# The projections of two head groups share one PSUM sum behind the last head, and half of the norms move behind it

## The chip, the cores and the metric

The kernel runs on one core of a Trainium2 chip. That core has five engines that work side by side, each on its own queue of instructions: TensorE (PE in the profile, its weight loads PEld) multiplies matrices and writes to PSUM; VectorE (DVE), ScalarE (ACT) and GpSimd (POOL) work on elements; SyncE (SP) issues the DMAs. The metric is the device time of one execution in microseconds, the median of several runs.

## The reference

A transformer encoder of two layers, 1024 tokens of width 1024, float32. Each layer mixes four groups of four heads side by side, joins their outputs through one output matrix, and follows it by a gated MLP with a convolution over tokens:

```python
for l in range(DEPTH):
    h = rms_norm(x, mix_pre_gain[l])
    (a_q, a_k, a_v, b_cq, b_ckv, b_kr, c_q, c_k, c_v, d_q, d_k, d_v) = split_columns(h @ w_in[l])
    o_a = neighbourhood_attention_2d(...)       # group a: 2-D window, learned relative bias
    ...
    mixed = jnp.concatenate([o_a, o_b, o_c, o_d], axis=-1) @ w_out[l]
    x = x + rms_norm(mixed, mix_post_gain[l])
    h = rms_norm(x, ffn_pre_gain[l])
    y = conv_gated_mlp(h, w_up[l], conv_w[l], conv_b[l], w_down[l])
    x = x + rms_norm(y, ffn_post_gain[l])
```

`mixed` is a sum over the groups: 256 columns of the concatenation, times 256 rows of `w_out`, for each. The order in which the groups' shares are added is free.

## The kernel before

Every float32 product is made of three matmuls of 128x512 (`mm3`, lines 255 to 257): each operand is split into a high part that TensorE takes at full rate and the low rest, ACT casting the high part and DVE subtracting it; `whi`/`wlo`, `PTh`/`PTl` are such pairs.

A layer runs through the input projection, the sixteen heads (groups d, c, b, a in this order), a *tail*, the *gated* part and the *down* part. Within the heads nothing is ordered by hand instruction by instruction: each step is put on a list with a planned time (`self.at(t, f)`), the steps are issued in the order of those times, and the numbers of the table `P` set them. A head takes four slots of the planned length `LD`, `LC`, `LB` or `LA` (5.4 for group a).

In a slot of group a, PE makes scores (`s_a`), DVE adds the relative bias and takes maxima (`P_a`, `nm_a`, line 1096), ACT exponentiates, POOL multiplies by `rr_a` (line 1134), PE transposes (`pt_a`, line 1183), ACT and DVE split the result into `PTh_a` and `PTl_a` (line 1193), and PE multiplies by the values (`ob_mix`, line 1210). The bias table comes by small DMAs and two POOL operations (lines 1016 and 1018, `rel_bias`).

The output projection of a finished group runs among the next group's heads. For each of eight tiles of 128 tokens and each half of 512 columns, `out_group`'s `mm` puts six matmuls into a PSUM bank (`ob`, `oc`, `oa` or `pb_mix`), and its `add` lets DVE add them to the running sum `y` (line 828). So group b's share is added among the heads of group a. Group a's own share comes behind the last head, in `tail`.

`tail` takes the token tiles one after another. Per tile: matmuls and two adds; ACT squares `y`, POOL takes the power (line 86, `rs_p`), and `y` is multiplied by the post gain (line 303, on DVE, for tile 5 on POOL); DVE adds it to the residual (`xo`, line 309); ACT squares again, POOL takes the power (`rs_f`); DVE makes the normed row (line 717). Then `split` transposes it and splits it into the operands `B11`, `B21` and `B22` of the gated part (`fB`, lines 274 to 276).

The gated part multiplies by 22 tiles of the up weights, by a scheme of seven products (P1 to P7) in place of eight, like Strassen's. It needs sums of token tiles (`token_sums`, line 757) and, from these, four more operands T1 to T4 (`fT`). T1, T2 and T4 lie in a pool that is opened when the mixing pool is closed; B11 and B21 lie in two of four *shared places* (`share(2)`, `share(3)`) that all parts use in turn. The first weight tile runs in two halves of 256 columns, `halves`.

The down part loads the gated rows and the down weights from HBM in pieces (`rows`), each into a place as it comes free: shared places 1, 2 and 3, and `fx` and `fy` of a pool that follows the gated part's.

## Time and profile before

| | us |
|---|---|
| median of 3 runs (2689.8 to 2691.87) | 2690.39 |
| the profiled execution | 2694.25 |
| its span, first to last instruction | 2692.4 |

Times on the page and in the rows count from the start of the span. A layer takes some 1336 us, and the second repeats the first. In an answer of the trace the engine named in brackets is the one that released the waiting instruction last; names are those of the program with their numbers left out.

### The profile page before, as it was taken

To read this page: it belongs to the slowest core of one execution; us is meant where nothing else is said; L and a number is where in the kernel's file an instruction comes from. 1 tells how busy PE (TensorE), PEld (TensorE's weight loads), DVE (VectorE), ACT (ScalarE), POOL (GpSimd) and SP (SyncE) were. 2 spreads that over 40 slices of the span, in tenths; PEclk is the share of its full clock that TensorE was granted. 3 is DMA by queue.
4 is the path that set the end of the run, shared out by engine and by line. 5 is a ranking of instruction groups with operands and counts; after the bars stand their busy time and mean duration, and the time that the engine had idled before them with its cause. 6 is when DMAs were issued, how large, how long until landed. Compare 5 with 4: busy or idle time off the path is not lost. (4 is left out here: it accounts for less than half of the span.)

```text
span 2692.4 us, 40234 instructions
## 1 busy us (share of the span) xinstructions
PE 2565.2 (95%) x14533; PEld 2210.0 (82%) x14533; DVE 2111.1 (78%) x3099; ACT 1463.6 (54%) x2704; POOL 798.2 (30%) x761
## 2 busy tenths in 40 slices
PE   7999999997799999999999999999968999999998
PEld 7999888885688888788789998888757888888886
DVE  5347899989878888878854568999797778888787
ACT  5347677666544444544653466776664444454433
POOL 1343212264333343100234432112743333330001
PEclk9999999999899999999999999999988999999999
DMA  6343412234222222550352434122432222226502
...
DMA packets 316913, 268.00 MB, mean 100 GB/s; under 512 B 104762, under 2 KB 262570, under 8 KB 316714
## 3 DMA queue, kind: packets, MB, share of 16 engines
...
## 5 line engine op out<-in xcount | busy, mean ns | idle before, releaser
L1309 POOL TENSOR_TENSOR sums<-loads 128x512 f32<-128x512 f32 x84 | 170.0, 2023 | 153.0 <-DMA loads<-in_w_up 67.2
L1309 POOL TENSOR_TENSOR loads<-loads,sums 128x512 f32<-128x512 f32 x42 | 57.7, 1374 | 372.4 <-DVE wgl L1319 229.5
L1530 ACT CAST dhP<-rows 128x1024 fp32r<-128x1024 f32 x88 | 89.4, 1052 | 130.1 <-issue 53.7
L86 POOL TENSOR_TENSOR rs_pf<-rs_pf,mhalf 128x1 f32<-128x1 f32 x15 | 13.9, 928 | 467.7 <-ACT rs_pf L85 467.6
L1531 DVE TENSOR_TENSOR dlP<-rows,dhP 128x1024 fp32r<-128x1024 f32 x88 | 105.2, 1219 | 40.7 <-ACT dhP L1530 40.7
L255 PE MATMUL dx<-dhP 128*128 128x512 f32 x308 | 120.2, 390 | 1.1 <-DVE yfQ L1597 1.1
L257 PE MATMUL dx<-dhP,dlP 128*128 128x512 f32 x308 | 120.0, 389 | 0.0
L256 PE MATMUL dx<-dlP,dhP 128*128 128x512 f32 x308 | 119.8, 389 | 0.0
L1188 ACT CAST PTh_b<-pt_b 128x512 fp32r<-128x512 f32 x128 | 74.9, 587 | 57.6 <-PE pt_b L1183 56.5
L257 PE MATMUL ux<-fT,wql 128*128 128x512 f32 (+1 forms) x272 | 102.6, 377 | 0.0
L255 PE MATMUL pb_mix<-whi_wa,h 128*128 128x256 f32 x320 | 100.0, 313 | 0.1
L1376 ACT ACTIVATE c<-ug,cw 128x1024 f32<-128x1024 f32 x44 | 54.7, 1244 | 82.4 <-DMA gate<-c 79.4
L255 PE MATMUL ux<-fT,wqh 128*128 128x512 f32 (+1 forms) x256 | 96.9, 378 | 1.4 <-ACT fT L275 1.4
L1377 DVE SCALAR_TENSOR_TENSOR c<-ug,cw,c 128x1023 f32<-128x1023 f32 x44 | 56.8, 1291 | 51.4 <-ACT c L1376 51.4
L256 PE MATMUL ux<-fT,wqh 128*128 128x512 f32 (+1 forms) x256 | 96.5, 377 | 0.0
L1419 ACT ACTIVATE c<-c 128x1024 f32<-128x1024 f32 x44 | 46.7, 1062 | 85.7 <-DVE c L1379 85.7
L1193 DVE TENSOR_TENSOR PTl_c<-pt_c,PTh_c 128x512 fp32r<-128x512 f32 x128 | 85.5, 682 | 8.5 <-ACT PTh_c L1188 7.9
L1188 ACT CAST PTh_c<-pt_c 128x512 fp32r<-128x512 f32 x128 | 74.5, 587 | 32.4 <-PE pt_c L1183 30.6
L1193 DVE TENSOR_TENSOR PTl_b<-pt_b,PTh_b 128x512 fp32r<-128x512 f32 x128 | 87.0, 683 | 6.3 <-ACT PTh_b L1188 5.4
L1028 PE MATMUL s_b<-rK,rQ 128*128 128x512 f32 x256 | 91.5, 414 | 0.4 <-ACT P_b L1105 0.4
L257 PE MATMUL pb_mix<-whi_wa,h 128*128 128x256 f32 x320 | 90.3, 282 | 0.0
L256 PE MATMUL pb_mix<-wlo_wa,h 128*128 128x256 f32 x320 | 90.3, 282 | 0.0
...
## 6 DMA issues: line engine op xcount, KB each, us to landing
...
```

The costliest lines, as they stand in the source:

```text
L255: nc.tensor.matmul(out, ah, bh, start=start and i == 0, stop=False, **flags)
L256: nc.tensor.matmul(out, ah, bl, start=False, stop=False, **flags)
L257: last = nc.tensor.matmul(out, al, bh, start=False, stop=stop and i == n - 1, **flags)
L1028: nc.tensor.matmul(out[:, c:c + w], Q[:, qt * 128:(qt + 1) * 128], K[:, k0 + c:k0 + c + w], start=i == 0, stop=i == len(ops) - 1)
L1188: nc.scalar.copy(x["sp"][0][:np, :n], x["pt"][:np, :n])
L1193: nc.vector.tensor_tensor(out=x["sp"][1][:np, :n], in0=x["pt"][:np, :n], in1=r32(x["sp"][0][:np, :n]), op=ALU.subtract)
L1309: nc.gpsimd.tensor_tensor(out=out, in0=a, in1=b, op=op)
L1376: nc.scalar.activation(c, u, AF.Identity, bias=b, scale=w1)
L1377: nc.vector.scalar_tensor_tensor(out=c[:, 1:], in0=u[:, :S - 1], scalar=w0, in1=c[:, 1:], op0=ALU.mult, op1=ALU.add)
L1419: nc.scalar.activation(a, a, AF.Gelu_apprx_tanh)
L1530: nc.scalar.copy(hi, src)
L1531: nc.vector.tensor_tensor(out=lo, in0=src, in1=r32(hi), op=ALU.subtract)
```

## The change

Group b's projection is no longer run among the heads of group a. For each token tile the tail takes one PSUM tile of 128x1024 (`oba`, one of two buffers), puts group b's twelve matmuls into it and then group a's twelve, and DVE adds it to `y` once. `LA` goes to 4.6, the DMAs of the relative bias (`load_bias`) are issued two slots ahead of the POOL work, and the tail's planned times are new.

The norms and splits of tiles 4 to 7 are collected in a list, `late`, and planned together with the first half of the first weight tile and the first token sums, inside `gated`. `y*post` runs on POOL for tiles 1 and 3. The mixing pool stays open through the gated part; B11, T1 and T2 are cut into pieces that fit its buffers (`parts`), each with a cast and a subtraction of its own in `operand`; T4 takes shared place 2 in B11's stead. The post gain is loaded later, behind the second `xo`, and `woa`'s second half is split later.

```diff
-    LD=5.39, LC=7.77, LB=8.59, LA=5.4,
+    LD=5.39, LC=7.77, LB=8.59, LA=4.6,
...
-    TP=1.65, T0=6.47, M1=2.84, X1=7.33, M2=7.77, X2=9.08, TS=0.41, TT=0.71, TU=9.01,
+    TP=5.45, T0=3.7, M1=5.6, X1=9.2, M2=10.6, X2=13.2, X3=14.6, PG=(1, 3), PO=1.2, TQ=2.8, L0=16, LP=6, S0=33, H0=36,
...
+                if kind == "b":
+                    continue
                 todo = [(t, i) for t in range(NT) for i in range(2)]
...
+                        if slot == 4 * m - 6:
+                            self.at(t0, lambda hd=hs[m]: self.load_bias(hd))
...
-            def mm(i):
-                f["mm"](t, i)
-
-            def add(i):
-                f["add"](t, i)
+            def mm(g):
+                if not g:
+                    x["ps"] = self.ps2(f"oba{tag}")
+                for i in range(2):
+                    (fb, f)[g]["part"](x["ps"][:, i * 512:i * 512 + 512], t, i, start=not g, stop=bool(g),
+                                       skip_group_check=True)
+
+            def add():
                 x["y"] = self.y[t // 4][:, t % 4, :]
...
+                nc.vector.tensor_tensor(out=x["y"], in0=x["y"], in1=x["ps"], op=ALU.add)
...
-                x["rs"] = self.square(r32(junk("jk")), x["y"], f"p{tag}", x["y"], self.post, None if t == 5 else nc.vector)
+                junk = self.wp.tile([128, NT, 128], F32R, tag="qs", name=f"jk{tag}", bufs=1).rearrange("p a b -> p (a b)")
+                x["rs"] = self.square(r32(junk), x["y"], f"p{tag}", x["y"], self.post, None if t in P["PG"] else nc.vector)
...
-                    for nm, i in (("B11", 2), ("B21", 3)):
-                        w = self.share(i, F32R, f"f{nm}{l}", (2, 4, 512))
-                        ops[nm] = w[:, 0], w[:, 1]
...
+                    ops["B11"] = self.parts(f"fB11{l}", (2, "P", NP), (2, "P", NP))
+                    w = self.share(3, F32R, f"fB21{l}", (2, 4, 512))
...
-            for dt, g in ((0, lambda: mm(0)), (0.8, lambda: add(0)), (0.9, lambda: mm(1)), (1.7, lambda: add(1)), (P["M1"], ms1),
-                          (P["X1"], xnew), (P["M2"], ms2), (P["X2"], xn)):
+            for dt, g in ((0, lambda: mm(0)), (2.7, lambda: mm(1)), (5.5, add)):
                 self.at(T + dt, g)
...
+            for dt, g in ((P["M1"], ms1), (P["X1"], xnew), (P["M2"], ms2), (P["X2"], xn), (P["X3"], split)):
+                if t < 4:
+                    self.at(T + dt, g)
+                else:
+                    late.append((P["L0"] + (t - 4) * P["LP"] + dt, g))
...
+        for k0, hi, lo in dst:
+            p = pt[:, k0:k0 + hi.shape[1], :]
+            nc.scalar.copy(hi[:, :, cols], p)
+            nc.vector.tensor_tensor(out=lo[:, :, cols], in0=p, in1=r32(hi[:, :, cols]), op=ALU.subtract)
...
-        with tc.tile_pool(name=f"fu{l}", bufs=1, reuse_waits="tile") as pool:
-            for nm in ("T1", "T2", "T4"):
-                w = pool.tile([128, 2, 4, 512], F32R, tag=nm, name=f"f{nm}{l}")
-                ops[nm] = w[:, 0], w[:, 1]
+        with self.mp:
+            pool = self.ap
+            ops["T1"] = self.parts(f"fT1{l}", (2, "P", NP), (1, "PT", NPT), (1, "PT", NPT))
+            ops["T2"] = self.parts(f"fT2{l}", (2, "aux", 4), (2, "aux", 4))
...
+            w = self.share(2, F32R, f"fT4{l}", (2, 4, 512))
...
-            for i in range(2):
-                halves[0][i]()
-            for i in range(2):
-                sums(i)
-            for i in (2, 3):
-                halves[0][i]()
+            down, self.events = self.events, []
+            for dt, f in ([(P["S0"] + 3 * i, lambda i=i: sums(i)) for i in range(2)] +
+                          [(P["H0"] + dt, halves[0][i]) for i, dt in enumerate((0, 2, 6, 11))] + late):
+                self.at(dt, f)
+            self.emit()
+            self.events = down
```

PE's queue among the heads of group a, before the change, in the second head (`s_a` scores, `pt_a` transposes, `ob_mix` the product with the values):

```order
L1072 MATMUL s_a_1_2_0_7658<-rK_2271,rQ_2270 128x320 x2
L256 MATMUL pb_mix_74<-wlo_wob_0_7535,o_4176 128x512
L1183 MATMUL pt_a_1_0_1_7694<-idf,P_a_1_0_0_7472 120x128 x3
L257 MATMUL pb_mix_74<-whi_wob_0_7534,o_4176 128x512
L1210 MATMUL ob_mix_73<-PTh_a_1_0_0_7627,rV_2272 128x256 x2
L1210 MATMUL ob_mix_73<-PTl_a_1_0_0_7628,rV_2272 128x256 x2
L1183 MATMUL pt_a_1_1_0_7736<-idf,P_a_1_1_0_7568 120x128 x4
```

The same place in the changed kernel:

```order
L1110 MATMUL s_a_1_2_0_7659<-rK_2271,rQ_2270 128x320 x2
L1221 MATMUL pt_a_1_0_1_7685<-idf,P_a_1_0_0_7480 120x128 x3
L1221 MATMUL pt_a_1_1_0_7715<-idf,P_a_1_1_0_7576 120x128 x4
L1110 MATMUL s_a_2_0_0_7785<-rK_2271,rQ_2270 128x320
L1248 MATMUL ob_mix_73<-PTh_a_1_0_0_7628,rV_2272 128x256 x2
L1248 MATMUL ob_mix_73<-PTl_a_1_0_0_7629,rV_2272 128x256 x2
```

The matmuls on `wob`, here two of `pb_mix`, are gone from between the head's own, and the third head's first score (`s_a_2_0`) stands earlier.

DVE's queue in the tail, before, from tile 4's second add on (`pb_mix` and `oa` carry the first and second half of group a's share, `fB` is an operand of the gated part):

```order
L828 TENSOR_TENSOR y_1_4175<-y_1_4175,oa_8584 128x512
L828 TENSOR_TENSOR y_1_4175<-y_1_4175,pb_mix_74 128x512
L717 SCALAR_TENSOR_TENSOR y_0_4174<-xo_3_8575,rs_f_3_8623,pre_8279 128x1024
L303 TENSOR_TENSOR y_1_4175<-y_1_4175,post_8277 128x1024
L276 TENSOR_TENSOR fB22V_8594<-pt_fB_1_0_8642,fB22Q_8593 128x4x128
L828 TENSOR_TENSOR y_1_4175<-y_1_4175,oa_8628 128x512
L828 TENSOR_TENSOR y_1_4175<-y_1_4175,pb_mix_74 128x512
L309 SCALAR_TENSOR_TENSOR xo_4_8619<-y_1_4175,rs_p_4_8637,xo_4_8619 128x1024
L828 TENSOR_TENSOR y_1_4175<-y_1_4175,oa_8660 128x512
```

In the changed kernel, from the last tile's add on:

```order
L712 TENSOR_TENSOR y_1_4175<-y_1_4175,oba_7_8635 128x1024
L777 TENSOR_TENSOR fB22V_8448<-pt_fB_3_8664,fB22Q_8447 128x4x128
L1359 TENSOR_TENSOR ws_0_8714<-wu_0_0_8693,ws_0_8714 128x512
L303 TENSOR_TENSOR y_1_4175<-y_1_4175,post_8290 128x1024
L786 TENSOR_TENSOR y_0_4174<-y_0_4174 128x512
L309 SCALAR_TENSOR_TENSOR xo_4_8486<-y_1_4175,rs_p_4_8723,xo_4_8486 128x1024
L786 TENSOR_TENSOR y_0_4174<-y_0_4174 128x512 x3
L729 SCALAR_TENSOR_TENSOR y_1_4175<-xo_4_8486,rs_f_4_8731,pre_8170 128x1024
```

Tile 4's multiplication by the post gain (the row of L303) stood between the two adds of tile 5, and its residual (`xo_4`) between those of tile 6; both now stand behind the add of tile 7, and with them all that follows for tiles 5 to 7.

## Rows read from the trace of the kernel before

**Rows 1.** The page, part 1: busy time of each engine, its share of the span, its instructions.

```profile
PE 2565.2 (95%) x14533; PEld 2210.0 (82%) x14533; DVE 2111.1 (78%) x3099; ACT 1463.6 (54%) x2704; POOL 798.2 (30%) x761
```

**Rows 2.** Table by stretches of the seam in layer 0: the stretch and its length, busy us of each engine with the number of its instructions (PE, PEld, DVE, ACT, POOL), then the granted clock of PE, the DMA share and GB/s.

```profile
562.00:624.00 62.00, 57.36 (x356) 48.07 (x355) 49.81 (x123) 38.29 (x92) 42.30 (x60) 1.00 0.42 112
...
636.00:713.00 77.00, 54.57 (x328) 45.68 (x327) 70.43 (x91) 42.92 (x87) 21.58 (x21) 0.87 0.24 89
```

**Rows 3.** The same table at the seam of layer 1, 1336 us later.

```profile
1898.00:1960.00 62.00, 57.60 (x349) 48.45 (x348) 48.81 (x120) 37.32 (x90) 40.15 (x58) 0.97 0.41 109
...
1972.00:2049.00 77.00, 56.79 (x323) 47.77 (x321) 69.90 (x90) 42.45 (x87) 21.57 (x21) 0.82 0.24 89
```

**Rows 4.** The same table in steps of 10 us, layer 0.

```profile
560.00:570.00 10.00, 9.30 (x63) 7.45 (x62) 9.02 (x20) 7.14 (x16) 9.64 (x16) 1.00 0.31 67
...
580.00:590.00 10.00, 9.98 (x62) 8.43 (x61) 8.01 (x23) 6.32 (x18) 6.17 (x11) 1.00 0.29 67
...
660.00:670.00 10.00, 5.97 (x30) 4.51 (x30) 9.98 (x13) 7.40 (x16) 5.15 (x5) 0.91 0.27 108
670.00:680.00 10.00, 4.07 (x16) 3.00 (x16) 8.51 (x9) 5.38 (x12) 4.26 (x5) 0.50 0.50 195
```

**Rows 5.** Groups of instructions by line, shapes kept apart, from 560.7 to 623 us: the count, busy us and mean ns of one, then the idle time before them.

```profile
L255 PE MATMUL ob<-whi_wob,o 128*128 128x512 f32 x16 | 6.7, 421 | 0.1
...
L828 DVE TENSOR_TENSOR y<-y,pb_mix 128x512 f32<-128x512 f32 x8 | 5.4, 671 | 0.0
```

**Rows 6.** DVE in order of time (start us, duration us, instruction, in brackets the idle time before it and what ended it).

```profile
560.74 0.54 DVE L1193 TENSOR_TENSOR PTl_a<-pt_a,PTh_a 120x384 fp32r<-120x384 f32 x1
...
610.14 0.49 DVE L1096 CUSTOM_DVE_ANT_0 P_a<-s_a,bias 128x320 f32<-128x320 f32 x1 [1.40 <-POOL bias L1016]
...
622.97 0.54 DVE L1193 TENSOR_TENSOR PTl_a<-pt_a,PTh_a 120x384 fp32r<-120x384 f32 x1
623.45 0.69 DVE L828 TENSOR_TENSOR y<-y,ob 128x512 f32<-128x512 f32 x1
624.05 1.22 DVE L237 TENSOR_TENSOR wlo_woa<-raw_woa,whi_woa 128x1024 fp32r<-128x1024 f32 x1
...
635.47 0.55 DVE L1193 TENSOR_TENSOR PTl_a<-pt_a,PTh_a 120x384 fp32r<-120x384 f32 x1
```

**Rows 7.** PE in order of time, a wait at the last heads' scores.

```profile
610.70 0.67 PE L1072 MATMUL s_a<-rK,rQ 128*128 128x440 f32 x2 [1.72 <-DVE nm_a L1096]
```

**Rows 8.** Groups of DVE's instructions from 636 to 713 us, columns as in rows 5.

```profile
L309 DVE SCALAR_TENSOR_TENSOR xo<-y,rs_p,xo 128x1024 f32<-128x1024 f32 x8 | 10.2, 1280 | 0.5 <-DMA xo<-in_x 0.5
L757 DVE TENSOR_TENSOR y<-y 128x512 f32<-128x512 f32 x16 | 10.2, 683 | 0.0
...
L1370 DVE TENSOR_TENSOR ug<-ob_gated,p 128x256 f32<-128x256 f32 x1 | 0.4, 418 | 0.0
```

**Rows 9.** POOL in order of time: the multiplication by the post gain of tile 5.

```profile
662.91 2.40 POOL L303 TENSOR_TENSOR y<-y,post 128x1024 f32<-128x1024 f32 x1
```

**Rows 10.** DVE in order of time, the same multiplication of two other tiles.

```profile
664.35 2.05 DVE L303 TENSOR_TENSOR y<-y,post 128x1024 f32<-128x1024 f32 x1
...
669.41 1.23 DVE L303 TENSOR_TENSOR y<-y,post 128x1024 f32<-128x1024 f32 x1
```

**Rows 11.** PE in order of time at a granted clock of 0.50 to 0.57.

```profile
674.88 1.12 PE L274 MATMUL pt_fB<-idf,y 128*128 128x128 f32 x4 [1.02 <-DVE fB L276]
...
687.15 0.41 PE L256 MATMUL ux<-fB,wgh 128*128 128x256 f32 x1
```

**Rows 12.** Groups of DVE's instructions over the whole span: the add of 1024 columns out of PSUM in the down part.

```profile
L1597 DVE TENSOR_TENSOR yfK<-yfK,dx 128x1024 f32<-128x1024 f32 x12 | 14.4, 1212 | 0.0
```

**Rows 13.** PE in order of time, from the last `pt_fT` transposes to the first product of weight tile 2.

```profile
712.68 0.66 PE L274 MATMUL pt_fT<-idf,y 128*128 128x128 f32 x4
713.09 0.36 PE L257 MATMUL ux<-fT,wql 128*128 128x256 f32 x1
...
715.08 0.28 PE L255 MATMUL ux<-fT,wqh 128*128 128x256 f32 x1
...
729.28 0.50 PE L255 MATMUL ux<-fT,more 128*128 128x512 f32 x1 [1.06 <-ACT p L1361]
...
735.71 0.50 PE L255 MATMUL uy<-fB22Q,ws 128*128 128x512 f32 x1 [3.37 <-ACT p L1361]
...
742.88 0.39 PE L255 MATMUL ux<-fB,wgh 128*128 128x512 f32 x1
```

**Rows 14.** PE in order of time, the first matmuls of the down part behind the last one of the gated part (`ux`).

```profile
1129.32 0.39 PE L257 MATMUL ux<-fT,wvl 128*128 128x512 f32 x1
1129.55 0.39 PE L255 MATMUL ob_mix<-first 128*128 128x512 f32 x1
...
1130.00 0.39 PE L257 MATMUL ob_mix<-first 128*128 128x512 f32 x1
```

**Rows 15.** SP in order of time, a DMA issue for the down part's second place.

```profile
1112.23 0.68 SPq L1504 DMA_DIRECT2D rows<-in_w_down  x1
```

**Rows 16.** SP in order of time, DMA issues of the second weight tile.

```profile
713.36 1.01 SPq L1304 DMA_DIRECT2D loads<-in_w_up  x2
```

**Rows 17.** ACT in order of time, the cast behind those loads.

```profile
717.47 1.05 ACT L1318 CAST wgh<-loads 128x1024 fp32r<-128x1024 f32 x1 [0.23 <-DMA loads<-in_w_up]
```

**Rows 18.** ACT in order of time, the cast of the down part's second operand.

```profile
1119.00 1.05 ACT L1530 CAST first<-rows 128x1024 fp32r<-128x1024 f32 x1 [0.88 <-DMA rows<-in_w_down]
```

More of the change, by code (lines that the diff above doesn't have):

```diff
@@ L567, in mix @@
         nc, tc = self.nc, self.tc
-        with tc.tile_pool(name=f"mix{l}", bufs=1, reuse_waits="tile") as pool:
-            self.ap = pool
+        self.mp = ExitStack()
+        pool = self.ap = self.mp.enter_context(tc.tile_pool(name=f"mix{l}", bufs=1, reuse_waits="tile"))
+        if True:
             self.nt = 5
@@ L683, in tail @@
         self.at(t0 - (64 - P["OE"]) * ln + 1.5, f["split"])
-        self.at(t0 - 4 * ln + 1, gains)
+        self.at(t0 - 4 * ln + 1, pre)
+        self.at(t0 - P["PO"] * ln, post)
+        late = []
         def tile(t, T):
@@ L712, in ms2 @@
                 x["new"] = 2
-                x["rs"] = self.square(r32(junk("jf")), x["xt"], f"f{tag}")
+                x["rs"] = self.square(x["y"], x["xt"], f"f{tag}")
             def xn():
@@ L730, in tile, with parts @@
             self.at(max(T - 8, Ts[t - 3] + 11) if t > 2 else T - 8, load)
[L731 to L732 removed]
+            for dt, g in ((0, lambda: mm(0)), (2.7, lambda: mm(1)), (5.5, add)):
                 self.at(T + dt, g)
[L734 to L736 removed]
+            for dt, g in ((P["M1"], ms1), (P["X1"], xnew), (P["M2"], ms2), (P["X2"], xn), (P["X3"], split)):
[3 more added lines that the diff above has]
+                    late.append((P["L0"] + (t - 4) * P["LP"] + dt, g))
+        T, Ts = 0, []
         for t in range(NT):
[L739 removed]
+            T = max(t0 - (2 - t // 4 * 2) * ln + P["T0"], T + (P["TP"] if t < 4 else P["TQ"]))
             Ts.append(T)
[L741 to L748 removed]
+            tile(t, T)
+        return ops, rows, late
+    def parts(self, name, *where):
+        k, out = 0, []
+        for n, tag, bufs in where:
+            out.append((k, *(self.ap.tile([128, n, 512], F32R, tag=tag, name=f"{name}{e}{k}", bufs=bufs) for e in "hl")))
+            k += n
+        return out
+    def operand(self, dst, i, src, tag):
+        nc = self.nc
+        pt = self.ps1([128, 4, 128], F32, f"pt_{tag}")
+        for j in range(4):
+            nc.tensor.transpose(pt[:, j, :], src[:, j * 128:(j + 1) * 128], self.idf)
+        cols = slice(i * 128, (i + 1) * 128)
+        for k0, hi, lo in dst:
+            p = pt[:, k0:k0 + hi.shape[1], :]
+            nc.scalar.copy(hi[:, :, cols], p)
+            nc.vector.tensor_tensor(out=lo[:, :, cols], in0=p, in1=r32(hi[:, :, cols]), op=ALU.subtract)
     def token_sums(self, e, o):
@@ L808, in split @@
         def split():
-            ws["w"] = [self.split_weights(x, f"wo{tag}_{i}") for i, x in enumerate(ws["raw"])]
+            ws["w"] = [self.split_weights(x, f"wo{tag}_{i}", *((self.ap, "P", NP) if kind == "a" and i else ()))
+                       for i, x in enumerate(ws["raw"])]
         def mm(t, i):
@@ L814, in mm, with part @@
             ws["ps", t, i] = ps = self.ps1([128, 512], F32, f"o{tag}") if bank is None else self.half(bank, True)
+            with self.begin(bank):
+                last = part(ps, t, i)
+            self.through(bank, last)
+        def part(ps, t, i, **flags):
             if kind == "a":
                 assert self.ow[kind, 2] == 4 and (kind, 3, t // 4 * 2 + 1) in self.ow
-            with self.begin(bank):
-                last = self.mm3(ps, [([x[:, t * 128:(t + 1) * 128] for x in ws["x"][k]], [x[:, k, :] for x in ws["w"][i]])
-                                     for k in range(2)])
-            self.through(bank, last)
+            return self.mm3(ps, [([x[:, t * 128:(t + 1) * 128] for x in ws["x"][k]], [x[:, k, :] for x in ws["w"][i]])
+                                 for k in range(2)], **flags)
         def add(t, i):
@@ L828, in add @@
                 nc.vector.tensor_tensor(out=y, in0=y, in1=ps, op=ALU.add)
-        return dict(load=load, raw=raw, split=split, mm=mm, add=add)
+        return dict(load=load, raw=raw, split=split, mm=mm, add=add, part=part)
     def slot(self, kind, n):
@@ L1003, in to_stack, with load_bias @@
         return [(0, tr), (0.4, out)]
+    def load_bias(self, hd):
+        nc, l, h = self.nc, hd["l"], hd["i"]
+        R = self.bias[:, 0, :24 * KC].rearrange("p (e a b) -> p e a b", e=2, b=KC)
+        for e in range(2):
+            for r in range(4):
+                base = 64 + ((l * 4 + h) * 15 + 3 - r) * 31 - 24 + 8 * e
+                nc.sync.dma_start(R[32 * r:32 * r + 32, e],
+                                  bass.AP(self.rpb.tensor, self.rpb.offset + base, [[1, 32], [31, 12], [1, KC]]))
     def rel_bias(self, hd):
@@ L1293, in slot @@
                 if isinstance(x, str):
-                    return self.wp.tile([128, D], F32R, tag=x, name=name, bufs=slots.count(x))
+                    return self.wp.tile([128, D], dtype, tag=x, name=name, bufs=slots.count(x))
                 return extra["more"][:, x]
@@ L1468, in ffn @@
     def ffn(self, l, h, x_src, x_dst):
+        ops, rows, late = h
         self.events = []
         plan = self.down(l, x_src, x_dst)
-        self.gated(l, *h)
+        self.gated(l, ops, rows, late)
         return plan()
```

50 lines of the change are left out of this document (22 added, 28 removed).

## The prediction

> **What bounds the kernel now.** First the page's busy shares [rows 1]: PE 95% of the span, DVE 78%. A kernel like this gains only where PE stands still or works slowly, so I next cut the seam between the heads of group a and the gated part into stretches. Layer 0 has it from 561 to 743 us, layer 1 about 1336 us later, and the two tables differ by 2.3 us at most in PE, DVE, ACT and POOL [rows 2, 3]; I work in layer 0 and count each result twice. The marks are DVE instructions found in both kernels: `PTl_a_0_0_1` at 560.74, `PTl_a_3_0_1` at 622.97, `PTl_a_3_3_1` at 635.47 [rows 6], and PE's last `pt_fT` transposes at 712.68 [rows 13].
>
> In the first stretch (62.2 us, twelve quarter-heads of group a) PE has 57.36 of 62.00 busy, POOL 42.30, DVE 49.81 and ACT 38.29 [rows 2]: PE is the bound. In the tail, 636 to 713, it is the other way: DVE 70.43 of 77.00, PE 54.57 [rows 2]. The ten-microsecond table shows both ends: PE 9.98 at 580, DVE 9.98 at 660, and at 670 PE down to 4.07 with the granted clock at 0.50, the lower of its two levels [rows 4]. Then PE waits on the chain that makes the second weight tile, until 742.88 [rows 13].
>
> **Part 1, the a-heads.** Removed are the 96 matmuls of group b's projection, 48 into `ob` and 48 into `pb_mix`, in three forms (16 of one form for `ob` [rows 5]). Consecutive 128x512 matmuls start 0.227 us apart (1129.32 to 1130.00 are three starts [rows 14]): 96 x 0.227 = 21.8 us of PE. Of the sixteen 128x512 adds, 15 lie in this stretch (the 8 out of `pb_mix` [rows 5], and all but one out of `ob`, which comes at 623.45); one takes 0.60 us to the start of the next (623.45 to 624.05 [rows 6]), 9.0 us of DVE. Left are PE 35.6, DVE 40.8, POOL 42.3, ACT 38.3. So no engine is the bound by itself; POOL comes nearest. One end: the planned slot goes from 5.4 to 4.6, and 62.2 x 4.6/5.4 = 53.0, a gain of 9.2. Other end: PE was kept 57.36/62 = 0.925 busy; if POOL were too, 42.3/0.925 = 45.7, a gain of 16.5. A piece is sure: the bias rows, now fetched two slots earlier, made DVE wait 1.40 us for POOL [rows 6] and PE 1.72 us for DVE's maxima behind it [rows 7]. I take the middle, **-13.0**.
>
> **Part 2, the last head's end** (12.5 us from `PTl_a_3_0_1` to `PTl_a_3_3_1`). PE has 25 projection matmuls there instead of 18: 7 x 0.227 = 1.6 us, if nothing of PE's idle time takes them. Between 0 and 1.6: **+0.7**.
>
> **Part 3, the tail.** It falls into two halves now. Up to the last sum `oba_7` PE sets the pace: 156 matmuls are left behind `PTl_a_3_3_1`, 156 x 0.227 = 35.4 us, and six transposes of four at 0.41 (712.68 to 713.09 [rows 13]), together 2.5: 37.9 us. DVE has only 28.5 us to do in it (six 128x1024 adds from PSUM, for which 1.21 is the nearest row [rows 12], four L309 and four L729, the old L717, at 1.28 [rows 8], sums, pieces). So DVE idles some 13 us, where it idled 6.6 in the whole tail [rows 2].
>
> POOL takes `y*post` for tiles 1 and 3, 2.40 us each [rows 9]; DVE's L309 of the tile waits for it, and the next sum's add stands behind L309 on DVE, so PE's two PSUM buffers run out. Bounds 0 and 4.8; I take 4.0, since the order puts the add right behind.
>
> A rule weighs against this move. When POOL multiplied at 662.91 to 665.31 [rows 9], DVE's own `y*post` begun at 664.35 took 2.05 us instead of 1.23 [rows 10]: 0.82 lost. The Trainium skill ("SBUF — State Buffer", Who interferes with whom) says that a VectorE instruction with two SBUF inputs contends with a GpSimd instruction that reads SBUF, and that the first one holds the shared port for the whole instruction. The trace nearly agrees: 665.31 plus 1.23 is 666.54, and 666.40 was measured. By the row the stall of one such DVE instruction stays under the 2.40; by the rule it could be all of it, 4.8 instead of 4.0 in a layer, and the total would be 1.6 us higher.
>
> Then the norms of tiles 4 to 7 follow with all operands behind them: by the built order one 1024-wide add and four L303 (5 x 1.14 from start to start), eight L309 and L729 (8 x 1.19), 26 of 512 columns (x 0.60), 21 of 256 (x 0.34 from 0.42 rows) and 8 of 128 (x 0.2, an estimate below the 256 row): 5.7 + 9.5 + 15.6 + 7.1 + 1.6 = 39.5. These are the durations of [rows 8] less the overlap of some 0.08 that neighbours show. Every tile's chain (square, POOL's power, L309, again) must be waited for; I add 6.0, near the 6.6 that DVE idled in all of the old tail. Sum 37.9 + 4.0 + 39.5 + 6.0 = 87.4 against 77.0: **+10.4**. If DVE's free time in the first half were used, it could be 5; if the clock falls, more (below).
>
> **Part 4, up to the third weight tile.** The chain of loads, casts and subtracts behind the last `y` is the same; PE stood 1.06 and 3.37 us in it [rows 13]. `ux_2`'s first product now stands ahead of the one that waited 3.37. Between 0 and -4.4: **-2.2**.
>
> **Part 5, into the down part.** T4 lies in shared place 2, where B11 lay. T4 is read by the last product of the last tile, which ends at 1129.55 [rows 14]; B11 was free 20 us earlier, and the second piece of `rows_2` was fetched at 1112.23 [rows 15]. PE has 12 matmuls of the other place ready (2.7 us, to 1132.3). The two loads can't be issued before 1129.6. The nearest landing in an empty queue is that of the 512 KB `loads`, issued at 713.36 [rows 16] and cast at 717.47 [rows 17]: 4.0. With a cast of 1.05 [rows 18] the operand is there at 1134.7: 2.4 us of PE. Half the bytes might land in half the time, 0.4 us. The other end is the busy queue: issued 1112.23 [rows 15], cast 1119.00 [rows 18], 6.8, or 5.2 us of PE. I take **+1.5**. The smaller pieces of T1, T2 and B11 are in the count of part 3. The late `post` load and the split of `woa_1` cost nothing while PE has `oba` matmuls of group b to do (22 us of them); without that cover a split is 1.05 + 1.22.
>
> **Sum**: -13.0 + 0.7 + 10.4 - 2.2 + 1.5 = -2.6 a layer, -5.2 in all. The profiled execution took 2694.25 us (span 2692.4, 1.85 around it), so it would be 2689.0 there; the median 2690.39 lies 3.9 lower, which gives **2685.2**. No change can be told from a change within 0.2%, 5.4 us.
>
> **Rivals.** (a) *The late norms fit in better*: DVE's 13 idle us in the first half take work of the second, the tail is 5 longer instead of 10.4: -8.0 a layer, 2674.4. For it: DVE was busy 9.98 of 10 in the old tail [rows 4], with the same operations to choose from. Against: the built order puts tile 4's multiplication behind `oba_7`'s add, and DVE works in that order.
>
> (b) *The clock eats it*. Four transposes took 1.12 us at the granted 0.50 and 0.66 at full clock, and a matmul of 256 columns 0.41 instead of 0.28 [rows 11, 13]; six groups of four and eight matmuls ran so between 671 and 688: 6 x 0.46 + 8 x 0.09 = 3.5 us. The second half is 45 us long with about as little for PE: 7.5, so 4 more a layer: +1.4, 2693.2.
>
> (c) *POOL becomes the bound of the a-heads* (slower). With 42.3 us of unchanged work POOL needs 0.75 busy even for 56.7 us; it works on the probabilities late in each quarter-head, and DVE's instructions beside it can lose time as in [rows 10]. Were the stretch only 5.5 shorter, the layer would be +4.9, **2700.2**; it decides from a gain below 7.7 on. For it: POOL 9.64 of 10 at 560 [rows 4]. Against: 6.17 at 580 with PE full, so POOL was waiting for PE there.
>
> (d) *It only moves*: the 21.8 us of PE cost behind the heads what they cost among them: 2690.4; I count it with (b).
>
> **How the numbers follow.** Forecast, 2679 to 2690: 0.38, of which 0.22 lie over 0.2% below. (a) 0.20. (b) with (d) 0.15, of which 0.02 slower by over 0.2%. (c) 0.27, of which 0.24 slower. Faster 0.22 + 0.20 = 0.42, slower 0.26, within 0.2% 0.32. The range leaves out about a tenth on each side. Its low end is (a) with part 1 at its other end, -16.5: -11.5 a layer, 2667. Its high end is (c) with part 5 at 2.5: +5.9 a layer, 2702.
>
> **What the profile would show.** Part 1: `PTl_a_0_0_1` to `PTl_a_3_0_1` in 49 us (53 or more speaks for (c), with POOL above 8 of 10 in each slice). Part 3: `oba_7`'s add 42 us behind `PTl_a_3_3_1`, the last `pt_fT` at 87; under 83 is (a), over 90 with a clock of 0.5 to 0.6 through the second half is (b). Part 5: PE idle 1 to 3 us at the thirteenth matmul of the down part, ended by ACT's `first`. Wrong above all would be parts 1 and 3, two large terms of opposite sign.

## The result: 1.5% slower, and the profile after

The changed kernel takes 2730.91 us (median of 4 runs, 2727.06 to 2734.35), the kernel before, run beside it, 2691.13; the ratio is 1.0148 (95% interval 1.013 to 1.0165). Forecast were 2685.2 and a range up to 2702, so the time lies 46 us above the forecast and 29 above the range. The profiled execution has a span of 2732.6 us, 40.2 more than before.

The page, part 1, of the changed kernel (before: [rows 1]):

```profile
PE 2589.3 (95%) x14533; PEld 2229.4 (82%) x14533; DVE 2103.7 (77%) x3081; ACT 1467.2 (54%) x2736; POOL 803.7 (29%) x763
```

The shares tell nothing: PE is 95% busy in both. The loss shows only in the stretches of the seam. First the marks, DVE in order of time (before: [rows 6]):

```profile
562.44 0.54 DVE L1231 TENSOR_TENSOR PTl_a<-pt_a,PTh_a 120x384 fp32r<-120x384 f32 x1
...
615.04 0.56 DVE L1231 TENSOR_TENSOR PTl_a<-pt_a,PTh_a 120x384 fp32r<-120x384 f32 x1
...
630.44 0.55 DVE L1231 TENSOR_TENSOR PTl_a<-pt_a,PTh_a 120x384 fp32r<-120x384 f32 x1
```

PE in order of time: the last `pt_fT` transposes, the first matmul of the down part, and the down part's first wait (before: [rows 13, 14]):

```profile
732.01 1.09 PE L772 MATMUL pt_fT<-idf,y 128*128 128x128 f32 x8 [0.18 <-DVE fT L777]
...
1149.75 0.39 PE L255 MATMUL ob_mix<-first 128*128 128x512 f32 x1
...
1155.71 0.80 PE L255 MATMUL ob_mix<-first 128*128 128x512 f32 x1 [3.08 <-ACT first L1576]
1156.30 0.63 PE L255 MATMUL pb_mix<-first 128*128 128x512 f32 x1
```

The table by stretches, columns as in [rows 2]: a-heads, last head's end, first half of the tail (to the add of `oba_7`), second half:

```profile
562.00:615.00 53.00, 41.81 (x275) 34.72 (x274) 40.16 (x104) 37.92 (x93) 39.34 (x59) 0.94 0.44 103
615.00:631.00 16.00, 14.22 (x83) 11.26 (x82) 12.40 (x25) 8.71 (x20) 7.89 (x8) 1.00 0.56 189
631.00:683.00 52.00, 43.25 (x193) 35.07 (x192) 35.59 (x34) 19.93 (x41) 17.07 (x14) 0.93 0.23 82
683.00:732.00 49.00, 37.20 (x210) 32.70 (x209) 38.47 (x64) 24.12 (x62) 5.07 (x8) 0.69 0.14 55
```

The terms of the sum, in us (the row of eight at 732.01 holds two groups, the last begins some 0.4 later; part 5 is what is left of a layer's shift up to the next mark):

| part | forecast | layer 0 | layer 1 |
|---|---|---|---|
| 1, a-heads | -13.0 | -9.6 | -10.4 |
| 2, last head's end | +0.7 | +2.9 | +2.9 |
| 3, tail | +10.4 | +24.7 | +22.8 |
| 4, to the down part | -2.2 | +0.5 | -2.8 |
| 5, into the down part | +1.5 | +2.3 | +5.2 |

With 1.7 us that layer 0 was late ahead of its first mark, these are the 40.2. Parts 1 and 2 together gave back 6.7 and 7.5 instead of 12.3; the tail took 24.7 instead of 10.4, and that is the larger miss. In the tail no engine is full: PE has 43.25 of 52 and 37.20 of 49, DVE 35.59 and 38.47. So it is made of waits. DVE in order of time in the first half:

```profile
644.39 1.28 DVE L309 SCALAR_TENSOR_TENSOR xo<-y,rs_p,xo 128x1024 f32<-128x1024 f32 x1 [4.55 <-POOL y L303]
...
655.81 1.77 DVE L786 TENSOR_TENSOR y<-y 128x512 f32<-128x512 f32 x1
...
660.37 2.27 DVE L309 SCALAR_TENSOR_TENSOR xo<-y,rs_p,xo 128x1024 f32<-128x1024 f32 x1 [2.18 <-POOL y L303]
662.56 1.75 DVE L786 TENSOR_TENSOR y<-y 128x512 f32<-128x512 f32 x1
664.23 1.21 DVE L712 TENSOR_TENSOR y<-y,oba 128x1024 f32<-128x1024 f32 x1
```

POOL in order of time beside it:

```profile
641.95 2.41 POOL L303 TENSOR_TENSOR y<-y,post 128x1024 f32<-128x1024 f32 x1
...
655.00 2.04 POOL L1349 TENSOR_TENSOR sums<-wu,wu 128x512 f32<-128x512 f32 x1 [0.42 <-ACT jk L300]
...
657.97 2.37 POOL L303 TENSOR_TENSOR y<-y,post 128x1024 f32<-128x1024 f32 x1
660.29 1.26 POOL L1349 TENSOR_TENSOR wu<-wu 128x512 f32<-128x512 f32 x1
661.63 2.13 POOL L1349 TENSOR_TENSOR sums<-wu,wu 128x512 f32<-128x512 f32 x1
```

PE behind DVE's add of 664.23:

```profile
665.49 0.79 PE L255 MATMUL oba<-whi_wob,o 128*128 128x512 f32 x1 [6.21 <-DVE y L712]
666.08 0.63 PE L256 MATMUL oba<-wlo_wob,o 128*128 128x512 f32 x1
666.51 0.63 PE L257 MATMUL oba<-whi_wob,o 128*128 128x512 f32 x1
```

DVE waits 4.55 and 2.18 us for POOL's two multiplications; the second one is late because POOL had the first gated weight tile's sums (655.00, 2.04) ahead of it, which in the kernel before came at 678.43. The next sum's add stands behind L309 on DVE, both PSUM buffers are full, and PE stands 6.21 us and comes back at the lower clock (granted 0.50 from 666 to 670): 0.43 from start to start instead of 0.227.

### The profile page after: what moved, and what is told of

It reads as the page before. It is cut to its first block, busy times and chain, and to the rows that moved or that the text cites. A ratio compares the mean times of both kernels' runs of the same rounds, so it can differ in the third digit from the quotient of the medians.

```text
span 2732.6 us, 40252 instructions
## 1 busy us (share of the span) xinstructions
PE 2589.3 (95%) x14533; PEld 2229.4 (82%) x14533; DVE 2103.7 (77%) x3081; ACT 1467.2 (54%) x2736; POOL 803.7 (29%) x763
## 3 DMA queue, kind: packets, MB, share of 16 engines
q8 instruction: 114, 1.87, 0.3%
## 5 line engine op out<-in xcount | busy, mean ns | idle before, releaser
L1422 DVE SCALAR_TENSOR_TENSOR c<-uv,cw,c 128x1023 f32<-128x1023 f32 x44 | 80.6, 1831 | 14.4 <-ACT c L1421 14.4
L1424 DVE SCALAR_TENSOR_TENSOR c<-uv,cw,c 128x1023 f32<-128x1023 f32 x44 | 88.3, 2008 | 0.4
L1479 DVE TENSOR_TENSOR c<-c,c 128x1024 f32<-128x1024 f32 x44 | 83.7, 1902 | 1.2
```

The source lines that it names most:

```text
L1422: nc.vector.scalar_tensor_tensor(out=c[:, 1:], in0=u[:, :S - 1], scalar=w0, in1=c[:, 1:], op0=ALU.mult, op1=ALU.add)
L1424: nc.vector.scalar_tensor_tensor(out=c[:, :S - 1], in0=u[:, 1:], scalar=w2, in1=c[:, :S - 1], op0=ALU.mult, op1=ALU.add)
L1479: nc.vector.tensor_tensor(out=a, in0=a, in1=c, op=ALU.mult)
```

## The experiments

All times are medians beside runs of the kernel before on the same chip (2689.6 to 2692.9); ratios are against that, with 95% intervals.

**Four single undoings.** *e1*: `PG=()`, DVE does all multiplications again. *e2*: nothing is deferred. *e3*: the place with T4 is refilled last. *e4*: the planned slot at its old length.

```
e1:  -    PG=(1, 3)                      +    PG=()
e2:  -    if t < 4: self.at(T + dt, g)   +    if t < 8: self.at(T + dt, g)
e3:  -    places = [(1, 2, 3, ...        +    places = [(1, 3, 2, ...
e4:  -    LA=4.6                         +    LA=5.4
```

> The changed kernel with one edit: y*post of all eight tiles on DVE, none on POOL. Theory 1 (POOL's multiplication stands in DVE's chain: DVE waited 4.55 and 2.18 us for it in layer 0, PE then 6.21 us for the add behind it, and PE's clock fell to half for some 6 us after): those waits go, DVE gets 2 x 1.14 us more work, so about 8 us a layer less: 2731 - 16 = 2715. Theory 2 (the norms of tiles 4 to 7 behind the last sum are what costs): the first half of the tail gets shorter by 3 us at most and the second stays 50: 2725 to 2731.

> The changed kernel with one edit: the norms and splits of tiles 4 to 7 are planned in the tail, each behind its own sum, as those of tiles 0 to 3, and nothing is left for the gated part. Theory 2 (deferral leaves PE idle and at half clock for 50 us behind the last sum, DVE idle for 20 us before it): DVE's work of the second half moves into the idle time of the first, about 10 us a layer less: 2731 - 20 = 2711. Theory 1 (POOL's multiplications): the stall at tile 3 stays and everything behind it moves with it, 2725 to 2731; more DVE work ahead of the sums could even make it slower.

> The changed kernel with one edit: the down part's first pairs take the shared places in the order 1, 3, 2, so that the place T4 lies in serves the third pair, not the second. PE waited 3.08 us (layer 0) and 2.65 us (layer 1) there for ACT's cast of the second pair, and ran at half clock for about 5 us behind it. If that wait is the whole cost: 3 to 5 us a layer less, 2731 - 8 = 2723. If the third pair only waits in its stead (it is needed 2.7 us later, and its cast is due 1.5 us after PE got there): 0 to -2, 2729 to 2731.

> The changed kernel with one edit: the planned slot of group a back to 5.4. If the shorter plan gave the gain in the a-heads (62.2 to 52.6 us in layer 0, 63.7 to 53.3 in layer 1), that stretch gets longer again, up to 5 us a layer: 2731 to 2741. If the gain comes only from the matmuls and adds that are gone, the plan's number matters little: 2728 to 2734. Third: the short plan overfills POOL and lets PE's clock fall at 590 to 600 (granted 0.63 to 0.69), then 5.4 is better by 2 to 6 us: 2725 to 2729.

Measured: e1 2716.54 (1.0096, 1.0079 to 1.0113), e2 2717.64 (1.0098, 1.0082 to 1.0113), e3 2726.62 (1.0135, 1.0119 to 1.015), e4 2731.08 (1.015, 1.0135 to 1.0165): 14.4, 13.3, 4.3 and 0 us of the 40. In e1 the tail's first half falls from 52.2 to 44.9 us and the second stays. So POOL's multiplications and the deferral each cost, neither alone explains the loss, and the planned slot length does nothing (e4).

**c1, the three together** (e1, e2 and e3 in one kernel).

> All three earlier edits at once: POOL multiplies nothing in the tail, no norm is deferred behind the PSUM change, and shared place 2 is the last to be refilled by the down part. Group b's projection stays behind the heads. Singly they gave 14.4, 13.3 and 4.3 us against the changed kernel (2730.9). If the causes are separate they add up: 2699. If the first two cure one and the same hold-up (the two PSUM buffers of the sums run out, PE stands, the clock falls), the second adds little: 2708 to 2714. Neither brings it below the 2690 of the kernel before; if it came there, the moved projection itself would be worth its price.

Measured 2700.85 (1.0037, 1.0024 to 1.005): 30.1 us, where the singles add up to 32.0. They add up to within 2 us, so they are separate causes. Of the change there are left the moved projection with its planned times, the kept pool and the early bias rows, and these are still 10 us slower than before.

**w1, the clock.** Ten matmuls with constant operands ahead of each group of four transposes of the late tiles and of the first three pairs' sums; the result is thrown away.

```
+    z = self.half("pb", True)[:, :256]
+    for k in range(10):
+        last = nc.tensor.matmul(z, warm[:, 0, :128], warm[:, 0, :256], start=True, stop=True, ...)
```

> The changed kernel with ten idle-work matmuls (256 columns, constant operands, result thrown away, 10 x 0.12 us) ahead of each group of four transposes of tiles 4 to 7 and of the first three pairs' sums, where PE stands in waits of 1.7 to 3.4 us and the granted clock is 0.50 from 695 to 715. Theory 'clock': with the clock held at 1.0, five rows of eight transposes take 1.25 instead of 1.94 us and some 35 matmuls of 256 columns 0.12 instead of 0.215 from start to start, 5 to 7 us a layer: 2717 to 2721. Theory 'chain': DVE's, ACT's and POOL's chain of the deferred norms sets the pace there and PE's half clock lies in its shade: 2729 to 2734, with the clock seen higher in the rows.

The table in steps of 10 us, first two rows of the changed kernel, then of w1:

```profile
690.00:700.00 10.00, 3.88 (x16) 3.14 (x16) 7.82 (x10) 5.86 (x16) 2.08 (x4) 0.54 0.30 105
700.00:710.00 10.00, 7.80 (x31) 6.30 (x31) 8.35 (x14) 5.01 (x13) 1.41 (x2) 0.50 0.14 56
```

```profile
690.00:700.00 10.00, 8.99 (x62) 8.81 (x62) 7.44 (x12) 5.08 (x13) 1.98 (x3) 0.83 0.32 107
700.00:710.00 10.00, 9.88 (x83) 9.73 (x84) 8.77 (x14) 6.70 (x17) 1.41 (x2) 1.00 0.17 65
```

The clock is back at 1.00 from 700 on (0.50 without the extra matmuls), and the time is 2731.10 (1.0145, 1.013 to 1.016), the same. With the deferral undone the second half takes 43.8 us, at a granted clock of 0.72 that is hardly better than the changed kernel's 0.69 (c1, in the tables of c1 and k7 further on). So the half clock isn't what makes the second half long. What does, DVE's rows tell: the last step of a tile's two norms (L729, in the kernel before L717), tiles 4 to 7. The kernel before:

```profile
670.56 1.28 DVE L717 SCALAR_TENSOR_TENSOR y<-xo,rs_f,pre 128x1024 f32<-128x1024 f32 x1
672.95 1.28 DVE L717 SCALAR_TENSOR_TENSOR y<-xo,rs_f,pre 128x1024 f32<-128x1024 f32 x1
677.08 1.28 DVE L717 SCALAR_TENSOR_TENSOR y<-xo,rs_f,pre 128x1024 f32<-128x1024 f32 x1
680.23 2.28 DVE L717 SCALAR_TENSOR_TENSOR y<-xo,rs_f,pre 128x1024 f32<-128x1024 f32 x1 [1.27 <-POOL rs_f L86]
```

The changed kernel:

```profile
690.10 1.28 DVE L729 SCALAR_TENSOR_TENSOR y<-xo,rs_f,pre 128x1024 f32<-128x1024 f32 x1 [1.25 <-POOL rs_f L86]
691.30 1.22 DVE L303 TENSOR_TENSOR y<-y,post 128x1024 f32<-128x1024 f32 x1
...
697.58 1.28 DVE L729 SCALAR_TENSOR_TENSOR y<-xo,rs_f,pre 128x1024 f32<-128x1024 f32 x1 [0.46 <-POOL rs_f L86]
...
705.41 1.28 DVE L729 SCALAR_TENSOR_TENSOR y<-xo,rs_f,pre 128x1024 f32<-128x1024 f32 x1 [0.40 <-POOL rs_f L86]
...
708.48 1.27 DVE L309 SCALAR_TENSOR_TENSOR xo<-y,rs_p,xo 128x1024 f32<-128x1024 f32 x1
...
713.04 1.28 DVE L729 SCALAR_TENSOR_TENSOR y<-xo,rs_f,pre 128x1024 f32<-128x1024 f32 x1 [1.37 <-POOL rs_f L86]
```

Before, the four tiles' chains overlap: one ends every 3.2 us in the mean. Deferred, the multiplication of a tile stands behind the last step of the tile before it (L303 at 691.30 behind L729 at 690.10), and each tile runs its whole chain (DVE, ACT's square, POOL's power, DVE) nearly alone: one every 7.6 us. In w1 they stand at 689.19, 697.15, 704.61 and 711.61, 7.5 apart in the mean with the clock up. So this chain sets the second half's pace.

PE isn't wholly out of it, and w1 doesn't measure the clock alone. ACT in the changed kernel:

```profile
710.36 0.59 ACT L776 CAST fT<-pt_fT 128x512 fp32r<-128x512 f32 x1 [0.27 <-PE pt_fT L772]
710.84 1.06 ACT L300 ACTIVATE y<-xo 128x1024 f32<-128x1024 f32 x1
```

Tile 7's square (710.84) begins 1.09 us behind the end of its L309 (708.48 + 1.27), because casts of transposes that ACT had to wait for stand ahead of it in ACT's queue. And PE in w1:

```profile
691.73 3.66 PE L774 MATMUL pb_gated<-fB22Q 128*128 128x256 f32 x18
695.22 0.60 PE L779 MATMUL pt_fT<-idf,y 128*128 128x128 f32 x4
```

Its extra matmuls hold up transposes here, which start no earlier than at half clock (695.16 in the changed kernel). From L729 to L729 it is 7.48, 7.83 and 7.63 us there, and 7.96, 7.46 and 7.00 in w1: some of what the clock gave back may have been paid for the extra matmuls. What the half clock costs by itself stays open. That the chain would be shorter with the four tiles closer in the event table wasn't tried.

**h1, the bias rows alone**, in the kernel before.

```
+    if slot == 4 * m - 6:
+        self.at(t0, lambda hd=hs[m]: self.load_bias(hd))
```

> The kernel before with one piece of the change alone: the bias rows of each head of group a fetched two quarter-heads earlier. The rows of before show DVE waiting 1.40 us for POOL's sum over those rows and PE 1.72 us behind it once a layer. If that wait lies on the path: 1.4 to 1.7 us a layer, 2686.5 to 2688. If the stretch is PE's and makes it good elsewhere: within 1 of 2690.

Measured 2686.68 against 2690.94 (0.9989, 0.9978 to 1.0): 4.3 us by the medians and 3.0 by the ratio, at the edge of what can be told. From `PTl_a_0_0_1` to `PTl_a_3_3_1` it takes 73.4 and 73.3 us instead of 74.7 and 76.2. This agrees with the 1.4 to 1.7 us a layer of [rows 6, 7] and doesn't settle them.

**f1 and f2, the projection back among the heads** (c1 with it there, the old slot and other planned times in the tail, `TP`, `T0`, `TQ`; f1 with the deferral, f2 without).

```
-    if kind == "b":
-        continue
```

> Group b's projection back among the heads of group a, as before the change, at the old slot length, POOL multiplying nothing, place 2 last; the kept pool, the earlier bias fetch and the norms of tiles 4 to 7 behind the PSUM change stay. The stretch from PTl_a_0_0_1 to PTl_a_3_3_1 should go back from 68 to 73 or 75 us. Theory 'deferral costs by itself': the second half of the tail stays some 50 us long and the first falls to 30, so the layer is 3 to 5 us worse than before: 2696 to 2700. Theory 'it is the moved projection': without it the tail is as short as before's: 2685 to 2691.

> As f1_b_in_heads_deferred, but nothing is deferred: of the change only the kept pool and the earlier bias fetch are left. Theory 'the moved projection and the deferral make the loss': 2684 to 2691, the bias wait of 1.4 to 1.7 us a layer gone. If the kept pool itself (smaller pieces, T4 in place 2) costs, it lies above 2695.

Measured 2714.32 (1.0081, 1.0066 to 1.0096) and 2714.51 (1.008, 1.0063 to 1.0097). f1 is far above what either theory said, and f2 far above its first; that it lies in the open range of its second proves nothing. They are no clean undoing, as DVE in f2 shows ahead of the last head's end:

```profile
632.88 1.23 DVE L1357 TENSOR_TENSOR wgl<-wu,wgh 128x1024 fp32r<-128x1024 f32 x1 [3.39 <-ACT wgh L1356]
```

The first gated weight tile's subtraction stands ahead of the head's last steps there, and DVE stood behind its load; the stretch from `PTl_a_0_0_1` to `PTl_a_3_3_1` grew to 80.4 us. What the kept pool costs by itself stays open.

**c3 and c5, the start of the gated part**: in c3 the first products come ahead of the pairs' sums (`S0=39` for 33, one apart), in c5 POOL's sums of the first weight tile are also held behind the last norm's power.

> c1_three_undone (2700.9) with the gated part's start in the order that the kernel before has: the first two products of the first weight tile, which need only the operands B11, B21 and B22, ahead of the pairs' sums and their transposes. In c1_three_undone PE stood 18 us between 672 and 699 and began its first product at 698.99, 32 us behind the last matmul of the sums but one; in the kernel before it began at 686.15, 19 us behind. Theory 'order': the products fill PE's waits, 2 to 4 us a layer, 2693 to 2697. Theory 'chain' (DVE's chain through the last norms ends as late as it did, whatever PE does in its waits): 2699 to 2703.

> c3_products_first with POOL's four sums over the first weight tile (1.26 to 2.13 us each, 7.8 in all with waits, 680.6 to 688.7 in c1_three_undone) held until POOL has done the last norm's small power; there DVE waited 3.0 us for that power behind them and PE 9.3 us for DVE. Theory 'POOL's queue again': 3 to 6 us a layer less than c3_products_first: 2685 to 2692. Theory 'other chain': the weight tile's third part comes later and PE waits for it instead: equal within 3, or worse.

Measured 2705.23 (1.0053, 1.0038 to 1.0069) and 2704.03 (1.0039, 1.0025 to 1.0053): no gain over c1's 2700.85. Neither the order of products and sums nor POOL's sums is worth what was hoped.

**c4, k7 and k8: how much to move.** c4 is c3, k7 is c1, each with group b's projection of tiles 0 to 3 among the heads again and only that of tiles 4 to 7 behind them; k8 keeps tiles 0 to 5 among the heads. Two planned times go with it in all kernels with such a share: the slot is 5.0, and tiles 0 to 3 of the tail follow each other after 2.8 us instead of 5.45 (`TP`).

```
-    if kind == "b":
-        continue
-    todo = [(t, i) for t in range(NT) for i in range(2)]
+    todo = [(t, i) for t in range(NT if kind != "b" else 4) for i in range(2)]
...
-    for i in range(2):
-        (fb, f)[g]["part"](..., start=not g, ...
+    for i in range(2) if g or t > 3 else ():
+        (fb, f)[g]["part"](..., start=not g or t < 4, ...
```

> c3_products_first with group b's projection of tiles 0 to 3 (48 of its 96 matmuls) among the heads of group a again, and only that of tiles 4 to 7 behind them; planned slot 5.0. PE has some 17 us idle in the 50 us of the heads' stretch when none of b's matmuls is there, and had 4.6 in 62 with all of them. Theory 'there is a best share': 48 x 0.227 = 10.9 us of PE go where half of it is free, the stretch grows by 3 to 6 and the tail's first half shrinks by 11: 5 to 8 us a layer better than c3_products_first, 2683 to 2690. Theory 'PE time is PE time': the stretch grows by 10, no change against c3_products_first within 4.

> c4_half_of_b_in_heads (2679.4) with the pairs' sums ahead of the first products again, as the change has them; without the half share that order was 4.4 us better (2700.9 against 2705.2). If that holds here: 2674 to 2677. If the difference there was noise of the schedule: 2678 to 2682.

> k7_half_b_sums_first with tiles 0 to 5 of group b's projection among the heads, and two tiles behind them. In c4_half_of_b_in_heads PE was 9.2 of 10 busy in the heads' stretch and DVE 10.0 of 10 in the tail from 640 to 670. So the 24 matmuls (5.4 us) should now lengthen the stretch by 3 to 5 and shorten the tail, which is DVE's, by less than 2: 1 to 4 us a layer worse than k7, 2678 to 2685. If the tail's first half is still PE's, it is 1 to 2 us a layer better than k7.

Measured: c4 2679.42 (0.9954, 0.9941 to 0.9966), k7 2681.41 (0.9966, 0.9954 to 0.9979), k8 2692.78 (1.0009, 1.0 to 1.0018). c4 beats both kernels, by 11.5 and 51.5 us, and is better than either of its theories; k7 is 2.0 slower with the other order; k8 is worse than both of its own. By stretches, c1 (a-heads and the tail's two halves):

```profile
563.00:617.00 54.00, 42.87 (x277) 35.75 (x277) 40.61 (x107) 38.36 (x94) 39.91 (x60) 0.94 0.45 109
...
632.00:679.00 47.00, 42.56 (x202) 34.87 (x200) 40.17 (x43) 23.14 (x52) 13.91 (x13) 0.97 0.36 126
679.00:723.00 44.00, 29.40 (x199) 27.17 (x200) 33.87 (x59) 21.83 (x52) 9.62 (x7) 0.72 0.06 25
```

k7, the same:

```profile
560.00:614.00 54.00, 49.05 (x317) 39.86 (x316) 44.70 (x115) 37.90 (x94) 40.03 (x60) 1.00 0.48 119
...
629.00:664.00 35.00, 33.45 (x165) 27.05 (x163) 34.28 (x37) 23.82 (x53) 14.03 (x13) 1.00 0.47 165
664.00:708.00 44.00, 30.23 (x205) 27.32 (x206) 38.12 (x64) 20.81 (x50) 11.00 (x7) 0.81 0.06 25
```

The marks, DVE in c1:

```profile
563.54 0.54 DVE L1231 TENSOR_TENSOR PTl_a<-pt_a,PTh_a 120x384 fp32r<-120x384 f32 x1
...
631.91 0.55 DVE L1231 TENSOR_TENSOR PTl_a<-pt_a,PTh_a 120x384 fp32r<-120x384 f32 x1
...
677.59 1.21 DVE L712 TENSOR_TENSOR y<-y,oba 128x1024 f32<-128x1024 f32 x1
```

And in k7:

```profile
560.45 0.54 DVE L1229 TENSOR_TENSOR PTl_a<-pt_a,PTh_a 120x384 fp32r<-120x384 f32 x1
...
628.56 0.55 DVE L1229 TENSOR_TENSOR PTl_a<-pt_a,PTh_a 120x384 fp32r<-120x384 f32 x1
...
662.56 1.21 DVE L710 TENSOR_TENSOR y<-y,oba 128x1024 f32<-128x1024 f32 x1
```

From `PTl_a_0_0_1` to `PTl_a_3_3_1` the time is 74.7 us with all of the projection among the heads (before; 73.4 in h1), 71.7 with three quarters (k8), 68.1 with half (k7) and 68.4 with none (c1). The first 48 matmuls to leave shorten it by 5 to 7 us, the other 48 by nothing: with them PE is busy 49.05 of 54 us, without them 42.87, so they had lain in PE's idle time. Behind the heads they are paid in full: the tail's first half is 46.9 us in c1 and 35.2 in k7, the second half 43.8 and 44.4. The other way, with three quarters among the heads, the heads take 3.6 us more than in k7 and the tail's first half isn't shorter (36.8 us): in k7 it is DVE's as well as PE's, 34.28 and 33.45 busy of 35. k7 and k8 differ in the share alone. So half is the best of the shares tried.

**k6 and k9, the other edits on half the move.** k6 is the changed kernel with the half share and its planned times, k9 is k7 with the deferral.

> The changed kernel with one edit: group b's projection of tiles 0 to 3 among the heads again (planned slot 5.0). POOL's two multiplications, the norms behind the PSUM change and the order of the shared places stay as the change has them. c4_half_of_b_in_heads had the heads' stretch up to PTl_a_3_3_1 at 67.6 us, as long as the changed kernel's 68.0, so the second half of the move bought nothing there. Theory 'the edits cost by themselves': the half share gives the 24 to 26 us that it gave c3_products_first, and the three others still cost what they cost singly: 2705 to 2708. Theory 'they cost because PE's matmuls fill the tail's first half': with half of them gone, POOL's multiplication is waited for less and the deferred norms have less to catch up: 2688 to 2696.

> k7_half_b_sums_first with the norms of tiles 4 to 7 behind the PSUM change again. Theory 'the deferral costs by itself', as it did with the whole projection behind the heads (13.3 us): 2687 to 2692, DVE idle in the tail's first half and the second half some 48 us long. Theory 'it costs only where PE sets the first half's pace': within 3 of k7.

Measured: k6 2706.48 (1.0058, 1.004 to 1.0076), k9 2693.80 (1.0009, 1.0 to 1.0018). "The edits cost by themselves" holds twice (k9 lies 1.8 us above that theory's range, k6 in it). The way from half the move to the changed kernel can now be walked in four kernels: k7 2681.4; with the deferral 2693.8 (+12.4); with POOL's multiplications and the order of places, k6, 2706.5 (+12.7); with the second half of the projection moved, the changed kernel, 2730.9 (+24.4). Without the other edits this last step is 19.4 (k7 to c1) or 25.8 (c4 to c3). The planned times `LA` and `TP` change with it; e4 shows that `LA` is worth nothing in the changed kernel, `TP` wasn't tried alone.

**r1 and r2, POOL among the heads.** c1 with the bias tables of the last two heads not made (r1 leaves them out and takes those of the head before), or made twice (r2), 9 us of POOL a layer.

```
r1:  +    if h in (2, 3):
     +        hd["bias"] = self.bias0
     +        return
r2:  +    for _ in range(1 + (h in (2, 3))):
```

> c1_three_undone (2700.9) with work left out: the last two heads of group a use the bias tables of the head before, so POOL does not make theirs (8 sums of 0.9 to 1.4 us a layer, 555 to 606, 9 us in all). Theory 'POOL is the bound of the heads once b's matmuls are gone' (rival (c)): the stretch from PTl_a_0_0_1 to PTl_a_3_3_1 falls from 68 to 60 or 63, 2685 to 2692. Theory 'a chain through several engines is' (POOL waits there for DVE's reciprocals, DVE for ACT's casts, PE for DVE's maxima): 67 to 68, 2698 to 2702.

> c1_three_undone with those same 8 sums of POOL done twice, 9 us more of POOL a layer. Theory 'POOL is the bound': the stretch grows from 68 to 74 or 77, 2712 to 2719. Theory 'chain': POOL has 10 us of waits there to take them up, the stretch grows by 0 to 3, 2700 to 2707.

Measured 2694.88 (1.0009, 1.0 to 1.0019) and 2704.77 (1.0052, 1.0036 to 1.0067), against c1's 2700.85: 3.0 us a layer less and 2.0 more. The stretch from `PTl_a_0_0_1` to `PTl_a_3_3_1` is 64.7 and 71.8 us in layer 0, c1's 68.4. Some third of POOL's time is in the path, the rest is not: r2 fits "chain" (2700 to 2707), r1 lies between the two theories. POOL takes part in a chain; it is not the bound.

## Why the prediction was wrong

The sum was built of busy times per engine, and failed where engines hand work to each other. The larger failure is part 3, +10.4 that became +24.7 and +22.8: its 37.9 for PE's sums measured 44.9, its 4.0 for POOL's multiplications 7.3 and its 6.0 for the chains' waits 10.5.

- **Part 1, oversized: -13.0 became -9.6 and -10.4.** The step that failed is "I take the middle" between 9.2 and 16.5: the low end, which came from the planned slots, was right to 0.4 in layer 0 and 1.2 in layer 1, but by luck, since the plan is not why (e4: the slot length does nothing). When b's matmuls are gone a chain through POOL, DVE, ACT and PE shows (r1, r2), and PE waits in it: 41.81 busy of 53. Rival (c) was near but not met: the stretch took 52.6 and 53.3 us, about its sign of 53, yet gained more than the 7.7 from which (c) decides, and POOL was busy 39.34 of 53, not above 8 of 10 in each slice; a third of POOL's time counts (r1, r2). That the early bias rows were worth their 1.4 to 1.7 agrees with h1.
- **Part 2: +0.7 became +2.9.** The trace has 27 projection matmuls there for 17 before, ten more instead of seven, 2.3 us at 0.227. The rest, and whether the count is the cause at all, no run tells apart.
- **Part 3, the first half: 41.9 became 52.2.** Without POOL's multiplications (e1) it is 44.9, so two terms failed. "37.9" for PE is 7.0 short. In e1 PE's last sum matmul ends at 671.63, 42.1 us behind the mark: 165 matmuls began behind it instead of 156 (2.0 us), PE waited 1.30 for a sum's add, and 0.8 are not accounted for. The last add ends at 674.46, another 2.8 us on, because DVE had the first gated weight tile's subtractions ahead of it (L1359 at 669.85 and 672.11). And "Bounds 0 and 4.8; I take 4.0" for POOL's part is 7.3. The bound was no bound: it counted 2.40 for each multiplication, and left out POOL's queue ahead of the second one (the weight tile's sums), DVE's instructions slowed beside POOL, and PE's half clock behind the 6.21 us.
- **The rule beside it.** L786 at 655.81 took 1.77 us beside POOL's sum that ended at 657.04: 657.04 + 0.68 is 657.72, it ended at 657.58. L786 at 662.56 likewise: 663.76 + 0.68 is 664.44, it ended at 664.31. Both lost what was left of POOL's instruction. The Trainium skill ("SBUF — State Buffer", Who interferes with whom) says that the first one holds the shared port for the whole instruction; these rows agree to 0.15 us. The 4.8 in place of 4.0 that the prediction drew from it was the better value and still too small, since the wait for the result and the queue ahead of it weigh more.
- **Part 3, the second half: 45.5 became 49.7.** DVE's work was forecast at 39.5 and is 38.47. "I add 6.0" for the waits became 10.5. The sentence behind it ("Every tile's chain must be waited for") named the cause and priced it by the old tail, where four chains overlap; deferred they come one after the other, 7.6 us each.
- **Rival (b), the clock, is seen in part and isn't the cause.** The tail took 102 us, over its 90, with 0.69 granted over the second half and 0.54 from 690 to 720, where (b) has 0.5 to 0.6 throughout. Yet w1, at 0.97 over that half, takes the same time. Part of the 4 us a layer that (b) asks for may be hidden by w1's own matmuls; of part 3's miss of some 14, e1 and e2 each alone take back 7.2 and 6.6 a layer.
- **What was not thought of:** That the 21.8 us which leave the heads are not of one price. I took the move as one block. Half of it is worth 10 us against the kernel before (k7), bias rows included; the other half, with its planned times, costs 24 (k6 against the changed kernel).
- **Parts 4 and 5** together came to +2.8 and +2.4 against -0.7. Part 4's waits for ACT stayed, 1.87 and 2.60 us (at 753.23 and 757.25, in layer 1 as well) where it was 1.06 and 3.37; what made layer 1's -2.8 is not told by them. The down part's wait is 3.08 us instead of 2.4 and is followed by matmuls at half clock (0.43 from start to start, 1155.71 to about 1162), which part 5 left out. e3 moved that load and gave 2.1 a layer.
